# Strassen pairs of an FFN: weight loads ahead of state loads, states finished one pair later with four row buffers, and one two-bank PSUM tile for the first two products

## The chip, the cores and the metric

One core of one Trainium2 chip. The kernel is one decoder layer for a prompt of 512 tokens and 8 sample tokens (520 in all), in fp32. The metric is device time in microseconds of one execution; the time before is the median of three runs.

## The reference

```python
D_MODEL = 1024
...
    h2 = rmsnorm(x, norm2_w) * (1 + sc2) + sh2
    gt, up = jnp.split(h2 @ w_ffn_in, 2, axis=-1)
    x = x + g2 * ((jax.nn.silu(gt) * up) @ w_ffn_out)
```

The layer first has a pooling branch and a state-space branch; what matters here is its second half. `w_ffn_in` is 1024 x 5632: 22 columns of 128 for the gate and 22 for the up part. Beside the FFN the kernel finishes the recurrent states of the sample tokens, new state = old state x decay + outer product, which are an output (`ssm_sample`) and which nothing in the FFN reads:

```python
    def step(h, inp):
        st, dec = inp
        return h * dec[..., None, None] + st, h
```

## The kernel before

**fp32 from pieces.** A weight block of 128 x 1024 is loaded raw, cast on ScalarE to a high part (`hi`, or a name that ends in h) and subtracted from the raw one on VectorE for a low part (`lo`, or l). Every product takes three matmuls for each k of 128: hi·xh, hi·xl, lo·xh. Tokens stand in two halves of 260.

**Columns and pairs.** Column j of the FFN is its gate block g and its up block u. Columns 1 to 3, 8, 14, 20 and 21 are plain (`ffn`, L1446): 96 matmuls of 128x260. The 14 columns in `WINO` (4 to 19 without 8 and 14) are "Strassen pairs" (`wino`, L1554): g and u with the two token halves make a 2x2 block product, done with seven products of 12 matmuls, 84 in all. In PE's order they are g0, g1 (weights wg, made of g itself), x0 (wx), z0 (wz), y1 (wy), z1 (wz), y0 (wy). wx and wz come from sums and differences of quarters of g and u, which GpSimd makes in place in the raw buffers (L1530, L1531, L1536, L1537); wy is u as these steps have left it. The results are combined by adds on VectorE (L1573) into `f1` (u2), `f2` (u4) and the column's result tile `as`; the sum for y0, called the f2 add here, is the last. The copy of g0 to u2 is ScalarE's (L1577).

**What runs when.** In this stage every engine keeps the order in which the program is written (`manual_schedule`, L1314). During pair j the next pair's weights are made: `wino_third(j)` (wyuh, wyul for this pair's y1 and y0; one buffer each, so wyuh(j) waits for y0 of pair j-1), `wino_first(j+1)` (wxeh, wxel, two GpSimd steps, wghi, wglo, two GpSimd steps, then silu and multiply of column j-1, which were left over), `wino_second(j+1)` (wzhi, wzlo), and `pair_load(j+2)` issues the raw loads of g and u of 512 KB each on SP's queue. Raw buffers: three ("raw"), and one of their own for u of odd columns ("ur"). In the runs 9 to 13 and 15 to 19 one of the three holds the gate block of the plain column that follows (loaded by `ahead`, L1547), so two turn round.

**States.** A generator (`sample_states`) treats 32 blocks of state. A step A loads the block after next (L1343, L1344, on SP), multiplies on GpSimd (L1359) and makes the outer product on ScalarE (four instructions `ht`, L1365); a step B adds on VectorE (L1367) and stores by a GpSimd DMA (L1368). Each pair does an A behind the add of g1 and a B at its end; 13 blocks are treated in the pairs, the others after them. The blocks lie in unused result tiles as[19] to as[21], their vectors `bb` in as[17] and as[18].

**PSUM.** `main()` gives tiles of two banks (tag m, two buffers), `bank()` single banks (tag b, four buffers). In a pair x0 and y1 are the two halves of one main tile `m`; g0, g1, z0, z1 and y0 each take a bank.

Of the kernel before, what the change touches and what calls it, by code (L numbers as in the profile page):

```python
# [9 lines left out]
F32 = mybir.dt.float32  # L10
# [6 lines left out]
P = 128  # L17
T = 520
TP = 512
NS = 8  # L20
H2 = 260
# [23 lines left out]
NFS = 3  # L45
NU = 40
WINO = [j for j in range(4, 20) if j not in (8, 14)]
STATES = 17

SLICES = ((0, 1), (1, 3), (3, 5), (5, 7), (7, 8))  # L50
U_SH1, U_SC1, U_G1, U_SH2, U_SC2, U_G2 = (8 * i for i in range(6))
# [3 lines left out]
def tile_decoder(ctx: ExitStack, tc: tile.TileContext, I: dict, O: dict):  # L55
    nc = tc.nc
# [12 lines left out]
    def uid():  # L69
        count[0] += 1  # L70
        return count[0]
# [4 lines left out]
    def main():  # L76
        return pm.tile([P, 2, 512], F32, tag="m", name=f"m{uid()}")
# [8 lines left out]
    def halves(ap):  # L86
        return ap.rearrange("p (a b) -> p a b", a=2)
# [38 lines left out]
    def product(outs, w, k, xh, xl, first, last, c0=0):  # L126

        hi, lo = w
        for a, b, f, e in ((hi, xh, first, False), (hi, xl, False, False), (lo, xh, False, last)):
            for o, t0, t1 in outs:  # L130
                nc.tensor.matmul(o, a[:, k, c0 : c0 + P], b[:, t0:t1], start=f, stop=e)  # L131

    def both(ps):
        return [(ps[:, s, :H2], s * H2, (s + 1) * H2) for s in range(2)]
# [9 lines left out]
    def column(ws, xh, xl, between=None, outs=None):  # L144

        ps = outs or main()
        n = sum(w[0].shape[1] for w in ws)
        kk = 0
        for w in ws:
            for k in range(w[0].shape[1]):  # L150
                product(outs or both(ps), w, k, xh(kk), xl(kk), kk == 0, kk == n - 1)
                kk += 1
                if between:
                    between(kk)
        return ps
# [5 lines left out]
    G = {}  # L161
# [1163 lines left out]
    states = {}  # L1325
    NEARLY = STATES - WINO[0]

    def state_unit(n):

        return n // 4, 2 * (n % 4)  # L1330

    def state_load(n):
        if n >= 32:
            return
        g, b = state_unit(n)
        if n < NEARLY:
            h = G["as"][19 + n % 3][:, 0:TP].rearrange("p (b j n) -> p b j n", b=2, j=2)
            bb = G["as"][17 + n % 3 // 2][:, n % 3 % 2 * 256 :][:, 0:256].rearrange("p (b n) -> p b n", b=2)
        else:
            sp = G["hs"]  # L1340
            h = sp.tile([P, 2, 2, P], F32, tag="hs", name=f"hs{n}", bufs=4)
            bb = sp.tile([P, 2, P], F32, tag="bb", name=f"bb{n}", bufs=3)
        nc.sync.dma_start(out=h, in_=I["sssm"][g, :, b : b + 2])  # L1343
        nc.sync.dma_start(out=bb, in_=dbc[g, 0, b : b + 2].unsqueeze(0).broadcast_to([P, 2, P]))  # L1344
        states[n] = h, bb

    def sample_states():


        for n in range(2):  # L1350
            state_load(n)
        yield True
        for n in range(32):
            g, b = state_unit(n)
            if n >= NEARLY or n + 2 < NEARLY:
                state_load(n + 2)
            h, bb = states.pop(n)
            at = dtx[:, 1, 2 * g : 2 * g + 2, b : b + 2].rearrange("p j b -> p b j")
            nc.gpsimd.tensor_tensor(h, h, at.unsqueeze(3).broadcast_to([P, 2, 2, P]), ALU.mult)  # L1359
            t = G["ff"].tile([P, T], F32, tag="fs", name=f"ht{n}", bufs=NFS)[:, 0:TP]  # L1360
            t = t.rearrange("p (b j n) -> p b j n", b=2, j=2)
            for i in range(2):
                for j in range(2):
                    x = xds[:, 2 * g + j, b + i : b + i + 1]
                    nc.scalar.activation(t[:, i, j], bb[:, i], AF.Identity, bias=0.0, scale=x)  # L1365
            yield True
            nc.vector.tensor_tensor(h, h, t, ALU.add)  # L1367
            nc.gpsimd.dma_start(out=O["ssms"][g, :, b : b + 2], in_=h)  # L1368
            yield True

    def states_step():
        if "states" not in G:
            G["states"] = sample_states()
        return next(G["states"], False)

    class Scratch:

# [68 lines left out]
    def ffn(j):  # L1446
        def fn(wg, wu):
            xh, xl = (lambda k: G["hh"][:, k]), (lambda k: G["hl"][:, k])
            left()
            pg = column([wg], xh, xl)  # L1450
            if j + 1 in WINO:
                wino_first(j + 1)
                if WINO[0] < j < STATES:
                    states_step()
                pair_load(j + 2)
            pu = column([wu], xh, xl)
            if j + 1 in WINO:
                wino_second(j + 1)
                if WINO[0] < j < STATES:
                    states_step()  # L1460
            ffn_end(j, whole(pg), whole(pu))

        return fn
# [43 lines left out]
    def pair_load(n):  # L1507
        if n in WINO:
            u = I["wfi"][NF + n]
            if n % 2:  # L1510
                raw = G["we"].tile([P, KD, P], F32, tag="ur", name=f"ur{n}", bufs=1)
                nc.sync.dma_start(out=raw, in_=u)
            WW["raw", n] = load(I["wfi"][n]), raw if n % 2 else load(u)
        elif WINO[0] < n:
            ahead(len(W["made"]), 2)
# [5 lines left out]
    def wino_first(n, mult=None, silu=None):  # L1521


        if n in WINO:
            g, u = WW["raw", n]
            a11, a12, a21, a22 = g[:, 0:4], g[:, 4:8], u[:, 0:4], u[:, 4:8]
            WW["x", n] = [G["we"].tile([P, 4, P], F32R, tag=t, name=f"wx{t}{n}", bufs=2) for t in ("eh", "el")]
            split(*WW["x", n], a22)
            v = nc.gpsimd.tensor_tensor
            v(a22, a21, a22, ALU.add)  # L1530
            v(a21, a11, a21, ALU.subtract)  # L1531
        elif n <= WINO[-1]:
            ahead(len(W["made"]) + 1)
        if n in WINO:
            split(*wide(n, "g"), g)
            v(a11, a22, a11, ALU.subtract)  # L1536
            v(a12, a12, a11, ALU.subtract)  # L1537
        if silu:
            silu()
            mult()  # L1540

    def wino_second(n):

        if n in WINO:
            split(*wide(n, "z"), WW["raw", n][0])
        else:
            ahead(len(W["made"]) + 1, 1)  # L1547

    def wino_third(n):

        WW["y", n] = [G["we"].tile([P, KD, P], F32R, tag=t, name=f"wy{t}{n}", bufs=1) for t in ("uh", "ul")]
        split(*WW["y", n], WW.pop(("raw", n))[1])

    def wino(j):  # L1554
        def fn():
            f1, f2 = (G["ff"].tile([P, T], F32, tag="fs", name=f"fs{j}_{i}", bufs=NFS) for i in range(2))
            u2, u4 = f1[:, 0:H2], f2[:, H2:T]
            s = G["as"][j]
            sa, sb = s[:, 0:H2], s[:, H2:T]
            tt = G["tt"]  # L1560
            B = lambda r, c: (hblock("hh", r, c), hblock("hl", r, c))
            twice = lambda ap: ap.unsqueeze(1).broadcast_to([P, 2, H2])

            def mult(kind, half, x, o=None):
                hi, lo = WW[kind, j]
                o = bank()[:, 0:H2] if o is None else o
                for k in range(4):
                    q = 4 * half + k
                    for a, b, f, e in ((hi, x[0], k == 0, False), (hi, x[1], False, False), (lo, x[0], False, k == 3)):
                        nc.tensor.matmul(o, a[:, q], b[:, k], start=f, stop=e)  # L1570
                return o

            add = lambda out, a, b: nc.vector.tensor_tensor(out, a, b, ALU.add)  # L1573
            m = main()
            wino_third(j)
            wino_first(j + 1, *G.pop("left", ()))
            nc.scalar.copy(u2, mult("g", 0, B(0, 0)))  # L1577
            add(sa, mult("g", 1, B(1, 0)), u2)
            if j < STATES:
                states_step()  # L1580
            pair_load(j + 2)
            mult("x", 0, tt[3], m[:, 0, 0:H2])
            add(u2, mult("z", 0, tt[1]), u2)
            mult("y", 1, tt[0], m[:, 1, 0:H2])
            add(halves(f2), m[:, :, 0:H2], twice(u2))
            add(sb, mult("z", 1, B(1, 1)), u4)
            wino_second(j + 1)
            add(halves(f2), twice(mult("y", 0, tt[2])), halves(f2))
            if j < STATES:
                states_step()  # L1590
            G["left"] = (
                lambda: nc.vector.tensor_tensor(s, f2, s, ALU.mult),
                lambda: nc.scalar.activation(s, s, AF.Silu, bias=0.0, scale=1.0),
            )
            for kind in "gxyz":
                WW.pop((kind, j))

        return fn
# [238 lines left out]
```

## Time and profile before

| | us |
|---|---|
| median of three runs | 1111.27 (1110.36 to 1113.66) |
| the profiled execution | 1116.53 |
| its span in the trace | 1114.7 |
| pairs 4 to 7 (758.88 to 804.31) | 45.43 |
| pairs 9 to 13 (815.85 to 877.74) | 61.89 |
| pairs 15 to 19 (889.28 to 951.12) | 61.84 |

Times in rows are microseconds from the start of the span. PE is TensorE's matmuls, PEld its weight loads, DVE VectorE, ACT ScalarE, POOL GpSimd, SPq the queue of SyncE that issues the DMAs. A row of the timeline has start, duration, engine, line, operation, output<-input (buffer numbers left out), partitions x elements, and in brackets how long the engine had been idle and what ended it. PEclk is the granted clock of TensorE as a share of full speed. Two following starts on one engine can be closer than a duration, since an instruction's end overlaps the next one's start; where a chain on one engine is summed, the distance of starts is used.

### The profile page before, as it was taken

To read this page: it belongs to the slowest core of one execution; us is meant where nothing else is said; L and a number is where in the kernel's file an instruction comes from. 1 tells how busy PE (TensorE), PEld (TensorE's weight loads), DVE (VectorE), ACT (ScalarE), POOL (GpSimd) and SP (SyncE) were. 2 spreads that over 40 slices of the span, in tenths; PEclk is the share of its full clock that TensorE was granted. 3 is DMA by queue.
4 is the path that set the end of the run, shared out by engine and by line. 5 is a ranking of instruction groups with operands and counts; after the bars stand their busy time and mean duration, and the time that the engine had idled before them with its cause. 6 is when DMAs were issued, how large, how long until landed. Compare 5 with 4: busy or idle time off the path is not lost.

```text
span 1114.7 us, 22415 instructions
## 1 busy us (share of the span) xinstructions
PE 1068.8 (96%) x9163; PEld 1034.6 (93%) x9163; DVE 767.9 (69%) x1111; ACT 528.1 (47%) x952; POOL 319.8 (29%) x436
## 2 busy tenths in 40 slices
PE   7988999999999999999999999999998988999996
PEld 6987999999999999999998999899888988999996
DVE  5686787877877798788577645586756667845442
ACT  4358464664664534845333333633434444655430
POOL 1133344243243441000000000366555554032211
PEclk7998999999999999999999999999999999999998
DMA  9435454534634523454444354223443423386632
GB/s 355 187 91 173 132 161 123 190 106 132 190 106 133 164 92 124 151 171 144 152 142 156 128 187 175 79 102 130 152 160 126 157 95 99 106 269 212 210 95 77
DMA packets 63590, 165.36 MB, mean 148 GB/s; under 512 B 10880, under 2 KB 20608, under 8 KB 62720
## 3 DMA queue, kind: packets, MB, share of 16 engines
q1 hardware_dynamic: 60928, 155.54, 42.7%
q0 software_dynamic: 2560, 8.39, 1.9%
q8 instruction: 72, 1.18, 0.4%
q14 instruction: 30, 0.25, 0.1%
HBM read 151.05 MB, written 12.86 MB: 147 GB/s over the span
## 4 chain that ended last, share of the span: by engine, by line
PE 67%; DMA 8%; POOL 8%; DVE 6%; ACT 5%; issue 4%; SPq 1%; POOLq 0%; ACTq 0%; DVEq 0%
PE m L131 54%; PE b L131 4%; DMA raw<-in_wfi 2%; DMA raw<-in_win 2%; POOL raw L1536 2%; PE b L1570 1%; PE b L797 1%; POOL raw L1537 1%; DMA araw<-in_wada 1%; DMA ur<-in_wfi 1%; DMA araw<-in_wad 1%; PE b L772 1%; PE b L799 1%; ACT wzhi L158 1%; PE b L209 1%
## 5 line engine op out<-in xcount | busy, mean ns | idle before, releaser
L131 PE MATMUL m<-hh,whi 128*128 128x260 f32 (+2 forms) x1392 | 292.0, 289 | 3.6 <-ACT v L646 3.5
L131 PE MATMUL m<-hh,wlo 128*128 128x260 f32 (+2 forms) x1392 | 285.2, 285 | 0.4 <-DVE wlo L119 0.3
L131 PE MATMUL m<-hl,whi 128*128 128x260 f32 (+2 forms) x1392 | 285.0, 284 | 0.3 <-DVE hl L483 0.2
L119 DVE TENSOR_TENSOR wlo<-raw,whi 128x1024 fp32r<-128x1024 f32 (+1 forms) x138 | 175.5, 1276 | 79.9 <-ACT whi L118 77.1
L131 PEld LDWEIGHTS m<-hh,whi 128*128 128x128 f32 x1392 | 218.1, 190 | 9.6 <-ACT v L646 3.7
L131 PEld LDWEIGHTS m<-hh,wlo 128*128 128x128 f32 x1392 | 217.9, 190 | 0.8 <-DVE wlo L119 0.8
L131 PEld LDWEIGHTS m<-hl,whi 128*128 128x128 f32 x1392 | 217.8, 190 | 0.7 <-DVE hl L483 0.4
L118 ACT CAST whi<-raw 128x1024 fp32r<-128x1024 f32 (+1 forms) x138 | 140.4, 1022 | 155.8 <-PE m L131 125.5
L654 DVE SCALAR_TENSOR_TENSOR v<-xb,cwh,v 128x512 f32<-128x512 f32 x96 | 72.5, 756 | 39.9 <-POOL xb L641 19.6
L343 POOL TENSOR_TENSOR r<-me,mhalf 128x5 f32<-128x5 f32 (+2 forms) x6 | 6.4, 1065 | 279.4 <-DVE me L342 279.4
L645 ACT COPY xb<-m 128x520 f32<-128x520 f32 (+1 forms) x31 | 17.9, 577 | 81.7 <-PE m L131 81.7
L131 PE MATMUL m<-ah,whi 128*128 128x260 f32 x264 | 53.2, 283 | 0.0
L131 PE MATMUL m<-al,whi 128*128 128x260 f32 x264 | 53.2, 283 | 0.0
L131 PE MATMUL m<-ah,wlo 128*128 128x260 f32 x264 | 53.1, 282 | 0.0
L131 PE MATMUL m<-gh,whi 128*128 128x260 f32 x256 | 52.8, 288 | 0.0
L131 PE MATMUL m<-gl,whi 128*128 128x260 f32 x256 | 51.3, 282 | 0.0
L131 PE MATMUL m<-gh,wlo 128*128 128x260 f32 x256 | 51.3, 282 | 0.0
L818 POOL TENSOR_TENSOR h<-h,cc 128x1024 f32<-128x1024 f32 x16 | 39.0, 2437 | 27.9 <-DMA cc<-dbc 27.0
L158 ACT CAST wzhi<-raw 128x1024 fp32r<-128x1024 f32 x14 | 14.7, 1049 | 67.9 <-POOL raw L1537 67.9
L159 DVE TENSOR_TENSOR wzlo<-raw,wzhi 128x1024 fp32r<-128x1024 f32 x14 | 17.2, 1226 | 39.8 <-ACT wzhi L158 39.8
L288 DVE TENSOR_TENSOR ar<-araw,aw 128x1024 f32<-128x1024 f32 x24 | 29.4, 1224 | 18.6 <-ACT aw L287 18.4
L131 PEld LDWEIGHTS m<-gh,whi 128*128 128x128 f32 x256 | 39.2, 188 | 2.4 <-PE b L303 1.1
(389 smaller groups left out, 2562.0 us busy)
## 6 DMA issues: line engine op xcount, KB each, us to landing
raw<-in_win SPq DMA_DIRECT2D x73, 512.0 KB, 4.8
raw<-in_wfi SPq DMA_DIRECT2D x36, 512.0 KB, 4.3
araw<-in_wada SPq DMA_DIRECT2D x24, 512.0 KB, 4.1
h<-in_sssm SPq DMA_DIRECT2D x16, 512.0 KB, 4.0
raw<-in_wssd SPq DMA_DIRECT2D x16, 512.0 KB, 3.4
raw<-in_wfo SPq DMA_DIRECT2D x16, 512.0 KB, 3.9
araw<-in_wad SPq DMA_DIRECT2D x6, 1024.0 KB, 14.6
hs<-in_sssm SPq DMA_DIRECT2D x19, 256.0 KB, 4.3
```

The lines of the kernel that those rows point to most:

```text
L118: nc.scalar.copy(hi, raw)
L119: nc.vector.tensor_tensor(lo, raw, hi.bitcast(F32), ALU.subtract)
L131: nc.tensor.matmul(o, a[:, k, c0 : c0 + P], b[:, t0:t1], start=f, stop=e)
L158: nc.scalar.copy(hi, src)
L159: nc.vector.tensor_tensor(lo, src, hi.bitcast(F32), ALU.subtract)
L209: nc.tensor.matmul(ps[32 * i : 32 * i + 32, 0:n], sc[:, k], raw[:, n * i : n * i + n], start=first, stop=last)
L288: nc.vector.tensor_tensor(r, raws[n], w1, ALU.subtract)
L645: nc.scalar.copy(shape(xb[:, 3 + t0 : 3 + t1]), o)
L654: nc.vector.scalar_tensor_tensor(v[:, 0:TP], xb[:, k : k + TP], w(k), v[:, 0:TP], ALU.mult, ALU.add)
L772: nc.tensor.matmul(o, bm[:, cc], xde[:, cc].rearrange("p h d -> p (h d)"), start=True, stop=True)
L818: nc.gpsimd.tensor_tensor(h0, h0, cc.unsqueeze(2).broadcast_to([P, 4, 2, P]), ALU.mult)
L1536: v(a11, a22, a11, ALU.subtract)
```

## The change

1. `pair_load(j + 2)` moves to the front of a pair's work, ahead of `wino_first(j + 1)` and the state's step A, so on SP the weight loads stand ahead of the state loads.
2. The states take `states_unit(j)`: behind the add of g1, step B of the last pair's block and then step A of the next. Row buffers are as[18] to as[21] by turns, `bb` has a pool of its own with three buffers, and `STATES` is 18: 14 blocks in the pairs.
3. g0 and g1 go to the two halves of a main tile `mg`; the banks are left to z0, z1 and y0.
4. `wino_second(j + 1)` comes behind the f2 add of y0.

```diff
-STATES = 17
+STATES = 18
...
-            h = G["as"][19 + n % 3][:, 0:TP].rearrange("p (b j n) -> p b j n", b=2, j=2)
-            bb = G["as"][17 + n % 3 // 2][:, n % 3 % 2 * 256 :][:, 0:256].rearrange("p (b n) -> p b n", b=2)
+            h = G["as"][18 + n % 4][:, 0:TP].rearrange("p (b j n) -> p b j n", b=2, j=2)
+            bb = G["we"].tile([P, 2, P], F32, tag="bb", name=f"bb{n}", bufs=3)
...
+    def states_unit(j):
+
+        if WINO[0] < j <= STATES:
+            states_step()
+        if WINO[0] <= j < STATES:
+            states_step()
...
             if j + 1 in WINO:
                 wino_first(j + 1)
-                if WINO[0] < j < STATES:
-                    states_step()
                 pair_load(j + 2)
+                states_unit(j)
             pu = column([wu], xh, xl)
             if j + 1 in WINO:
                 wino_second(j + 1)
-                if WINO[0] < j < STATES:
-                    states_step()
...
-            m = main()
+            m, mg = main(), main()
             wino_third(j)
+            pair_load(j + 2)
             wino_first(j + 1, *G.pop("left", ()))
-            nc.scalar.copy(u2, mult("g", 0, B(0, 0)))
-            add(sa, mult("g", 1, B(1, 0)), u2)
-            if j < STATES:
-                states_step()
-            pair_load(j + 2)
+            nc.scalar.copy(u2, mult("g", 0, B(0, 0), mg[:, 0, 0:H2]))
+            add(sa, mult("g", 1, B(1, 0), mg[:, 1, 0:H2]), u2)
+            states_unit(j)
             mult("x", 0, tt[3], m[:, 0, 0:H2])
             add(u2, mult("z", 0, tt[1]), u2)
             mult("y", 1, tt[0], m[:, 1, 0:H2])
             add(halves(f2), m[:, :, 0:H2], twice(u2))
             add(sb, mult("z", 1, B(1, 1)), u4)
+            add(halves(f2), twice(mult("y", 0, tt[2])), halves(f2))
             wino_second(j + 1)
-            add(halves(f2), twice(mult("y", 0, tt[2])), halves(f2))
-            if j < STATES:
-                states_step()
```

Lines behind L1372 stand a few lines further down in the changed kernel (L1570 is L1574, L1573 and L1577 are L1577 and L1582).

**PE, from g0 to g1 of pair 10.** Names end in a number; b580 and b581 are banks, m575 is the two-bank tile `mg`, hh2 and hl2 are the tokens' high and low parts. A bracket lists the semaphores that an instruction waits for, by the engine that raises them. Before:

```order
L1570 MATMUL b580_10257<-hl2_8188,wghi10_10117 128x260
L1570 MATMUL b580_10257<-hh2_8187,wglo10_10118 128x260
L1570 MATMUL b581_10271<-hh2_8187,wghi10_10117 128x260 [waits DVE_49]
L1570 MATMUL b581_10271<-hl2_8188,wghi10_10117 128x260
L1570 MATMUL b581_10271<-hh2_8187,wglo10_10118 128x260
```

After:

```order
L1574 MATMUL m575_10240<-hl2_8188,wghi10_10123 128x260
L1574 MATMUL m575_10240<-hh2_8187,wglo10_10124 128x260
L1574 MATMUL m575_10240<-hh2_8187,wghi10_10123 128x260 [waits Activation_49]
L1574 MATMUL m575_10240<-hl2_8188,wghi10_10123 128x260
L1574 MATMUL m575_10240<-hh2_8187,wglo10_10124 128x260
```

The products stand in the same order; the first matmul of g1 waited for VectorE (a bank to be emptied) and now waits for ScalarE. The count that it waits for is that of the copy of g0 to u2, the same for which VectorE's add of g1 waits.

**ScalarE, pair 12 in the changed kernel.** The copy is fs12_0<-m588; in front of it are this pair's wyuh, the next pair's casts and the left-over silu of column 11, behind it the state's four instructions and wzhi.

```order
L158 CAST wyuh12_10509<-raw577_10247 128x1024
L158 CAST wxeh13_10515<-ur13_10379 128x512
L158 CAST wghi13_10521<-raw583_10381 128x1024
L1594 ACTIVATE as11_8986<-as11_8986 128x520
L1582 COPY fs12_0_10505<-m588_10508 128x260
L1365 ACTIVATE ht8_10561<-bb8_10291,xds_94 128x128 x4
L158 CAST wzhi13_10633<-raw583_10381 128x1024
```

Before, these seven stand in the same order; the copy read a bank, and ht read bb from as[18].

**VectorE, from the end of pair 9 into pair 10.** fs9_1 is f2 of pair 9, as9 its result, as21 and as18 hold states. Before:

```order
L1573 TENSOR_TENSOR as9_8984<-b577_10202,fs9_1_10105 128x260
L159 TENSOR_TENSOR wzlo10_10217<-raw569_10043,wzhi10_10216 128x1024
L1573 TENSOR_TENSOR fs9_1_10105<-b578_10220,fs9_1_10105 128x520
L1367 TENSOR_TENSOR as21_8996<-as21_8996,ht5_10154 128x512
L159 TENSOR_TENSOR wyul10_10240<-raw570_10045,wyuh10_10239 128x1024
L159 TENSOR_TENSOR wxel11_10244<-ur11_10159,wxeh11_10243 128x512
L159 TENSOR_TENSOR wglo11_10250<-raw575_10161,wghi11_10249 128x1024
```

After:

```order
L1577 TENSOR_TENSOR as9_8984<-b572_10205,fs9_1_10106 128x260
L1577 TENSOR_TENSOR fs9_1_10106<-b573_10219,fs9_1_10106 128x520
L159 TENSOR_TENSOR wzlo10_10234<-raw565_10035,wzhi10_10233 128x1024
L159 TENSOR_TENSOR wyul10_10242<-raw566_10037,wyuh10_10241 128x1024
L159 TENSOR_TENSOR wxel11_10250<-ur11_10113,wxeh11_10249 128x512
L159 TENSOR_TENSOR wglo11_10256<-raw570_10115,wghi11_10255 128x1024
```

The f2 add, which waits for y0, stands ahead of wzlo(10), and the state's add has gone to the next pair, behind the add of g1.

## The prediction

> **What bounds the kernel now.** First the page: where busy time goes, and whether one engine has all of it.
>
> ```profile
> PE 1068.8 (96%) x9163; PEld 1034.6 (93%) x9163; DVE 767.9 (69%) x1111; ACT 528.1 (47%) x952; POOL 319.8 (29%) x436
> ```
>
> TensorE (PE) is busy for 96% of the 1114.7 us span, so an edit that neither adds nor removes matmuls can only win or lose PE's idle time. The change touches columns 4 to 19 of the FFN, so I ask next for busy time by stretch: pairs 4 to 7, plain column 8, pairs 9 to 13, pairs 15 to 19, and last a short piece of pair 18.
>
> ```profile
> core 0: us, PE busy (x) PEld busy (x) DVE busy (x) ACT busy (x) POOL busy (x), PEclk, DMA share, GB/s
> 758.88:804.31 45.43, 41.99 (x339) 40.77 (x337) 32.04 (x40) 22.26 (x40) 26.35 (x20) 1.00 0.40 131
> 804.31:815.85 11.54, 11.54 (x98) 11.54 (x97) 5.47 (x8) 3.49 (x7) 5.79 (x5) 1.00 0.65 214
> 815.85:877.74 61.89, 55.11 (x423) 52.65 (x422) 43.84 (x52) 28.00 (x50) 33.18 (x28) 0.97 0.37 127
> 889.28:951.12 61.84, 54.95 (x422) 52.67 (x421) 40.51 (x51) 25.11 (x39) 29.36 (x23) 0.97 0.30 99
> 930.40:933.81 3.41, 3.41 (x18) 3.41 (x17) 2.00 (x3) 2.51 (x3) 0.73 (x1) 0.50 0.00 0
> ```
>
> The plain column keeps PE full: eight products of 12 matmuls in 11.54 us, so one product takes 1.44 us and a pair's seven 10.1 us. The 14 pairs take 45.43 + 61.89 + 61.84 = 169.2 us, where 14 x 10.1 = 141: PE waits for some 28 us. For what, the groups of weight loads say (the last column is PE's idle time before the group and what ended it).
>
> ```profile
> L1570 PEld LDWEIGHTS b<-hh,wghi 128*128 128x128 f32 x112 | 22.3, 200 | 7.2 <-DVE as L1573 7.1
> L1570 PEld LDWEIGHTS b<-t1h,wzlo 128*128 128x128 f32 x56 | 10.5, 188 | 3.9 <-DVE wzlo L159 3.9
> L1570 PEld LDWEIGHTS m<-t0h,wyul 128*128 128x128 f32 x56 | 10.5, 188 | 6.9 <-DVE wyul L159 6.9
> L1570 PEld LDWEIGHTS b<-t2h,wyuh 128*128 128x128 f32 x56 | 10.5, 188 | 4.4 <-ACT fs L1577 4.4
> ```
>
> There are two kinds of wait. The products g0 and y0 wait for a PSUM bank (until the add of g1, or the copy at L1577, has emptied one); z0 and y1 wait for weights. One turn of the weights, pair 4 into pair 5, on VectorE:
>
> ```profile
> 764.20 0.68 DVE L159 TENSOR_TENSOR wxel<-ur,wxeh 128x512 fp32r<-128x512 f32 x1
> ...
> 772.41 1.23 DVE L159 TENSOR_TENSOR wzlo<-raw,wzhi 128x1024 fp32r<-128x1024 f32 x1 [4.03 <-ACT wzhi L158]
> 773.56 0.69 DVE L1573 TENSOR_TENSOR fs<-b,fs 128x520 f32<-128x520 f32 x1
> 774.17 0.68 DVE L1367 TENSOR_TENSOR as<-as,ht 128x512 f32<-128x512 f32 x1
> 774.77 1.22 DVE L159 TENSOR_TENSOR wyul<-ur,wyuh 128x1024 fp32r<-128x1024 f32 x1
> 775.90 0.68 DVE L159 TENSOR_TENSOR wxel<-raw,wxeh 128x512 fp32r<-128x512 f32 x1
> ```
>
> From wxel to wxel is 11.70 us. GpSimd's four subtractions, wzhi, wzlo, the f2 add of y0, the state's add, wyul and wxel follow one another, and the change takes the f2 add (0.61) and the state's add (0.60) out from between. That is what it can win. Now what it adds.
>
> **The new wait.** In the built program the first matmul of g1 waits for ScalarE, for the very count that the add of g1 waits for: the copy of g0 to u2. g0 and g1 are now halves of one tile, and a write to the tile waits for a read of it. Before, g1 had a bank of its own, and of the pair's products only y0 came after that copy. So the question is how late the copy is. It stands on ScalarE behind wyuh(j), wxeh(j+1), wghi(j+1) and silu(j-1). Pairs 11 and 12, with PE's starts of each:
>
> ```profile
> 840.54 0.39 PE L1570 MATMUL b<-hh,wghi 128*128 128x260 f32 x1 [0.64 <-DVE as L1573]
> 854.45 0.39 PE L1570 MATMUL b<-hh,wghi 128*128 128x260 f32 x1 [1.79 <-DVE as L1573]
> ```
>
> ```profile
> 848.53 0.62 ACT L158 CAST wxeh<-raw 128x512 fp32r<-128x512 f32 x1 [3.83 <-DMA raw<-in_wfi]
> 849.06 1.05 ACT L158 CAST wghi<-raw 128x1024 fp32r<-128x1024 f32 x1
> 850.01 0.63 ACT L1593 ACTIVATE as<-as 128x520 f32<-128x520 f32 x1
> 850.54 0.35 ACT L1577 COPY fs<-b 128x260 f32<-128x260 f32 x1
> ...
> 862.35 1.05 ACT L158 CAST wghi<-raw 128x1024 fp32r<-128x1024 f32 x1 [3.26 <-DMA raw<-in_wfi]
> 863.31 0.64 ACT L1593 ACTIVATE as<-as 128x520 f32<-128x520 f32 x1
> 863.85 0.36 ACT L1577 COPY fs<-b 128x260 f32<-128x260 f32 x1
> ```
>
> The copy ends 10.35 and 9.76 us after g0's first matmul, and g0 takes 1.44. Before, PE used that time for five products; now everything behind g0 waits. And the load that holds the copy up isn't late for SP's order, which the change does improve: it waits for a buffer.
>
> ```profile
> 843.78 1.23 DVE L159 TENSOR_TENSOR wzlo<-raw,wzhi 128x1024 fp32r<-128x1024 f32 x1 [1.43 <-ACT wzhi L158]
> 844.92 0.69 DVE L1573 TENSOR_TENSOR fs<-b,fs 128x520 f32<-128x520 f32 x1
> ...
> 857.65 1.22 DVE L159 TENSOR_TENSOR wzlo<-raw,wzhi 128x1024 fp32r<-128x1024 f32 x1 [1.39 <-ACT wzhi L158]
> 858.80 0.69 DVE L1573 TENSOR_TENSOR fs<-b,fs 128x520 f32<-128x520 f32 x1
> ```
>
> ```profile
> 858.91 0.33 SPq L109 DMA_DIRECT2D raw<-in_wfi  x1
> ```
>
> SP issues the load 0.04 us after wzlo(12) ends at 858.87. Of three raw buffers one holds the preloaded weight of the next plain column in each run of five pairs, so two turn round, and the load for pair 13 goes where g(12) was until wzlo(12) had read it. The change then moves wzlo(j) on VectorE behind the f2 add, which waits for the last matmul of pair j-1. That closes a ring that PE itself stands in.
>
> **The sum, runs of five pairs.** Even pair j, from the end of y0(j-1): semaphores to VectorE and back to PE 0.3 (my estimate: two or three steps of the size of 858.87 to 858.91, rounded up), f2 add 0.61 (773.56 to 774.17), then from wzlo's start to the copy's end 864.21 - 857.65 = 6.56, then six products 6 x 1.44 = 8.64: 16.1 us. Odd pair: the load that waits is u's, and wxeh, which reads u, stands ahead of wghi: 850.89 - 843.78 = 7.11 in place of 6.56: 16.65. Last pair (13, 19): nothing to load, ScalarE has one wyuh (0.95), a cast of the plain column (0.95), silu (0.53) and the copy (0.36) from the end of y0 on: 2.8 + 0.3 + 8.64 = 11.7. First pair (9, 15): its turn begins in the plain column, as before:
>
> ```profile
> 824.19 0.36 ACT L1577 COPY fs<-b 128x260 f32<-128x260 f32 x1
> 898.29 0.36 ACT L1577 COPY fs<-b 128x260 f32<-128x260 f32 x1
> ```
>
> 824.55 - 815.85 = 8.70, + 8.64 = 17.3; and 898.65 - 889.28 = 9.37, + 8.64 = 18.0. The runs come to 17.3 + 16.1 + 16.65 + 16.1 + 11.7 = 77.9 (before 61.9: +16.0) and 18.0 + 16.1 + 16.65 + 16.1 + 11.7 = 78.6 (before 61.8: +16.7).
>
> **Pairs 4 to 7.** Here no raw buffer is held, and loads land in time. Pair 4:
>
> ```profile
> 758.88 0.28 PE L1570 MATMUL b<-hh,wghi 128*128 128x260 f32 x1
> ```
>
> ```profile
> 761.19 0.60 ACT L1397 ACTIVATE as<-m 128x520 f32<-128x520 f32 x1
> 764.09 0.38 ACT L1577 COPY fs<-b 128x260 f32<-128x260 f32 x1
> ```
>
> g0 now takes the PSUM tile that silu of plain column 3 reads until 761.79 (2.9 us of wait), and g1 the copy's end at 764.47: 5.6 + 8.64 = 14.2. Pairs 5 and 6: wyuh waits for the end of y0 (its tile has one buffer), then 0.95 + 0.53 + 0.95 + 0.53 + 0.36 = 3.3 to the copy's end, + 0.3 + 8.64 = 12.3 each; pair 7 as 13, 11.7. Sum 50.5, before 45.4: +5.1.
>
> **What lies beside.** The four row buffers, bb in a pool of its own and the state's add one pair later move work of 1 to 1.3 us an instruction off VectorE's urgent stretch; with PE waiting 2 to 6 us a pair for the copy, VectorE and GpSimd have that slack anyway, so I count 0. GpSimd's multiply still stands behind its subtractions. State loads behind weight loads on SP: 0 for the same reason, since the state is needed a pair later. One state more lies in the pairs and one fewer behind them, where the page shows PE at nine tenths or more: 0, at most its add, multiply and scaling, some 3 us, either way. Own banks for z0, z1, y0: y0 no longer waits for a bank, which the sums above hold already.
>
> **The clock.** The stretch 930.40 to 933.81 follows a stall of PE and shows PEclk 0.50, with 18 matmuls recorded in 3.41 us; at the plain column's pace 28 fit, so a hit costs up to 10 x 0.12 = 1.2 us.
>
> ```profile
> 913.39 0.39 PE L1570 MATMUL b<-t2h,wyuh 128*128 128x260 f32 x1 [1.19 <-ACT fs L1577]
> 929.02 0.39 PE L1570 MATMUL b<-hh,wghi 128*128 128x260 f32 x1 [1.78 <-DVE as L1573]
> ```
>
> The stall that it follows lasted 1.78 us; one of 1.19 wasn't followed by a slow stretch. The sums make eleven stalls of 2 to 7 us (four in each run of five, three in the first run): 0 to 13 us, and part of a slow stretch may fall into the stall itself, so I take half, 6 us. [...]
>
> **Total.** 16.0 + 16.7 + 5.1 + 6 = +43.8. The profiled execution took 1116.5 us (span 1114.7), 5.3 over the median of the runs shown, 1111.27, and within its own few tenths of a per cent of them; 1116.5 + 43.8 - 5.3 = 1155 us.
>
> **Rivals.** *The wait is there but the loads come in time* (SP's new order gets a free buffer sooner): every pair but the first of a run is then 12.3, the last 11.7: 50.5 + 66.0 + 66.7 = 183.2, +14, so 1125. For it: weight loads now go ahead of state loads. Against: 858.91, issued 0.04 us after wzlo. *The wait doesn't bite* (the chip or the build lets g1 go on before the copy): then the chain of weights bounds the pairs as before, and with wzlo behind the f2 add little is won: -2 to +2, 1111. Against: the wait is in the built program. [...] *Faster*: the copy is ready when g0 ends. It has to end within 1.44 us of g0's start, so wghi(j+1) must be cast before pair j begins and wyuh must not stand ahead. Then the ring of 11.70, less the two adds, decides: 14 x 10.5 = 147 against 169, -22, 1089. Against: all of the copies quoted end 5.6 us or more after g0's start. *Slower still*: clock hits at every stall (+7), and the loads that PE waits for share the queues with the state loads issued behind them; the lone load took 862.35 - 858.91 = 3.44, and the page's median for such loads is 4.3 us, so six of them cost +5: 1167.
>
> ```profile
> raw<-in_wfi SPq DMA_DIRECT2D x36, 512.0 KB, 4.3
> ```
>
> **How the numbers follow.** The forecast has 0.80, loads in time 0.09, no bite 0.05, faster 0.03, above 1172 0.03. The range is the forecast's own: down to 1137 without the clock (-6) and with three of the six middle pairs' loads in time (-3 x 4, from 16 to 12), up to 1167 of the last rival, + 3 for the state and 2 for scatter: 1172. The cases outside it hold 0.20. About 0.3% is what a measurement of this kernel can tell from no change; faster by more than that 0.03, within 0.05, slower 0.92.
>
> **What would show it.** Right: in the groups, PE's idle time before b<-hh,wghi goes, and a group of matmuls of wghi into m waits some 40 us or more, ended by ScalarE's fs copy; runs of five take 73 to 82 us; slow clock stretches in most pairs; PE idle before wyul and y0's wyuh near nothing. Wrong: g1 follows g0 without a gap, or wghi's cast is not preceded by a wait for raw<-in_wfi.

## The result and the profile after

| | before | after |
|---|---|---|
| median | 1110.98 us (four runs, 1110.36 to 1113.66) | 1166.97 us (four runs, 1165.45 to 1167.33) |
| the profiled execution | 1116.53 us | 1166.78 us |
| its span | 1114.7 us | 1164.9 us |

The change makes the kernel 4.96% slower: the ratio is 1.0496, 95% interval 1.0477 to 1.0516. The time lies in the range that was given (1137 to 1172), 12 us above the forecast.

The page of the changed kernel, first its busy times:

```profile
PE 1077.9 (93%) x9163; PEld 1046.4 (90%) x9163; DVE 773.6 (66%) x1111; ACT 530.2 (46%) x952; POOL 323.1 (28%) x436
```

The instruction counts are those of before, and VectorE, ScalarE and GpSimd are busy as long as they were, to 6 us. Of the 50 us of span, PE stands idle for 41 more than before (87.0 against 45.9) and is busy for 9 more, at a lower clock (granted on average over the span: 0.960 against 0.980). The three stretches of pairs, with the same columns as before (the first starts at the end of plain column 3, since g0 of pair 4 now waits):

```profile
757.35:808.57 51.22, 42.90 (x338) 41.80 (x337) 33.05 (x41) 23.64 (x42) 26.87 (x20) 0.97 0.40 133
820.19:905.19 85.00, 59.80 (x421) 58.75 (x421) 43.80 (x53) 27.97 (x50) 31.93 (x26) 0.82 0.33 109
916.80:999.68 82.88, 59.66 (x421) 58.60 (x421) 42.19 (x51) 25.49 (x41) 29.24 (x23) 0.84 0.24 80
```

45.43, 61.89 and 61.84 us have become 51.22, 85.00 and 82.88: +49.9 us, the whole difference of the spans. The mean clock falls from 0.97 and 0.97 to 0.82 and 0.84 in the runs of five. The groups of weight loads say what PE waits for; this is the only group of a pair in the changed kernel with a wait of note:

```profile
L1574 PEld LDWEIGHTS m<-hh,wghi 128*128 128x128 f32 x112 | 25.8, 230 | 60.2 <-ACT fs L1582 57.1 <-ACT as L1404 2.9
```

The four waits of before (7.2 for a bank, 3.9 for wzlo, 6.9 for wyul, 4.4 for the copy ahead of y0) are gone. In their place stand 57.1 us for the copy at L1582, and 2.9 us for silu of column 3. One turn, the end of pair 10 and pair 11, followed through VectorE, SP, ScalarE and PE:

```profile
856.16 0.70 DVE L1577 TENSOR_TENSOR fs<-b,fs 128x520 f32<-128x520 f32 x1 [1.01 <-PE b L1574]
856.78 1.22 DVE L159 TENSOR_TENSOR wzlo<-raw,wzhi 128x1024 fp32r<-128x1024 f32 x1
```

```profile
858.02 0.33 SPq L109 DMA_DIRECT2D raw<-in_wfi  x1
858.46 0.36 SPq L1343 DMA_DIRECT2D as<-in_sssm  x1
858.87 0.43 SPq L1344 DMA_DIRECT2D bb<-dbc  x1
```

```profile
862.14 0.62 ACT L158 CAST wxeh<-raw 128x512 fp32r<-128x512 f32 x1 [4.99 <-DMA raw<-in_wfi]
862.66 1.04 ACT L158 CAST wghi<-raw 128x1024 fp32r<-128x1024 f32 x1
863.61 0.63 ACT L1594 ACTIVATE as<-as 128x520 f32<-128x520 f32 x1
864.15 0.36 ACT L1582 COPY fs<-m 128x260 f32<-128x260 f32 x1
```

```profile
864.56 0.58 PE L1574 MATMUL m<-hh,wghi 128*128 128x260 f32 x1 [7.00 <-ACT fs L1582]
```

The f2 add starts when PE has finished y0 of pair 10; wzlo follows it; the load starts 0.02 us after wzlo has ended (858.00) and frees the buffer; ScalarE casts what has landed 4.12 us later; the copy ends at 864.51, and 0.05 us later g1 starts, after PE has stood for 7.00 us. Every step of the ring is in the rows, in the order that was forecast.

### The profile page after: what moved, and what is told of

It reads as the page before. It is cut to its first block, busy times and chain, and to the rows that moved or that the text cites. A ratio compares the mean times of both kernels' runs of the same rounds, so it can differ in the third digit from the quotient of the medians.

```text
span 1164.9 us, 22402 instructions
## 1 busy us (share of the span) xinstructions
PE 1077.9 (93%) x9163; PEld 1046.4 (90%) x9163; DVE 773.6 (66%) x1111; ACT 530.2 (46%) x952; POOL 323.1 (28%) x436
## 4 chain that ended last, share of the span: by engine, by line
PE 71%; DMA 9%; ACT 7%; DVE 6%; issue 4%; POOL 3%; SPq 0%; POOLq 0%; ACTq 0%; DVEq 0%
PE m L131 50%; PE m L1574 6%; PE b L1574 4%; DMA araw<-in_wada 4%; PE b L131 3%; DMA raw<-in_wfi 2%; PE b L797 2%; DVE ar L288 1%; PE b L772 1%; DMA araw<-in_wad 1%; PE b L799 1%; DMA raw<-in_win 1%; DVE wzlo L159 1%; ACT aw L287 1%; PE b L209 1%
## 5 line engine op out<-in xcount | busy, mean ns | idle before, releaser
L1574 PE MATMUL m<-hh,wghi 128*128 128x260 f32 x112 | 38.8, 346 | 56.7 <-ACT fs L1582 54.0
L1574 PEld LDWEIGHTS m<-hh,wghi 128*128 128x128 f32 x112 | 25.8, 230 | 60.2 <-ACT fs L1582 57.1
L1365 ACT ACTIVATE ht<-bb,xds 128x128 f32<-128x128 f32 x128 | 40.9, 391 | 20.8 <-DVE as L1593 20.6
L1577 DVE TENSOR_TENSOR fs<-b,fs 128x260 f32<-128x260 f32 (+1 forms) x28 | 15.8, 564 | 38.8 <-PE b L1574 38.8
```

## The experiments

Two theories stood against each other. A: the loss is the wait of g1 for the copy of g0, through the tile that both now share, and the copy is late because it stands on ScalarE behind casts of a load that waits for a raw buffer. B: the loss comes from the new order on the queues (wzlo behind the f2 add, the loads, the states). Every run is timed against the kernel before on the same chip; the ratios are to that.

### Parting the tile from the order

**e1_g1_bank**: g1 gets a bank of its own, the rest of the change stays.

```diff
-            add(sa, mult("g", 1, B(1, 0), mg[:, 1, 0:H2]), u2)
+            add(sa, mult("g", 1, B(1, 0)), u2)
```

> The change, but g1 writes a bank of its own; g0 keeps its tile. Theory A (the loss is g1's wait for a late copy, through the shared tile): the wait of some 58 us before wghi goes, the clock stays up, time within 1095 to 1118 us. Theory B (the loss is the new order: wzlo behind the f2 add, loads, states): still above 1140 us.

Measured: 1113.45 us, ratio 1.0006 (0.9995 to 1.0016). One line takes the loss away. In the groups of weight loads g0 (into its tile m) keeps its wait for silu, and g1 (into a bank b) waits for nothing but its bank:

```profile
L1574 PEld LDWEIGHTS b<-hh,wghi 128*128 128x128 f32 x56 | 11.1, 198 | 1.6 <-DVE as L1577 1.6
L1574 PEld LDWEIGHTS m<-hh,wghi 128*128 128x128 f32 x56 | 11.1, 197 | 4.1 <-ACT as L1404 3.0 <-ACT fs L1582 0.9
```

**e2_only_tile**: the kernel before with the shared tile and nothing else.

```diff
-            m = main()
+            m, mg = main(), main()
...
-            nc.scalar.copy(u2, mult("g", 0, B(0, 0)))
-            add(sa, mult("g", 1, B(1, 0)), u2)
+            nc.scalar.copy(u2, mult("g", 0, B(0, 0), mg[:, 0, 0:H2]))
+            add(sa, mult("g", 1, B(1, 0), mg[:, 1, 0:H2]), u2)
```

> The kernel before, with nothing but g0 and g1 in one two-bank tile. A: PE waits for ScalarE's copy in every pair; since wzlo still stands ahead of the f2 add the load comes sooner than in the change, so a pair takes between 12.3 us (load in time) and 16 (load late): 1125 to 1155 us. B: within 5 us of 1111.

Measured: 1155.97 us, ratio 1.0384 (1.0369 to 1.0400), 1 us above A's range. The wait ahead of wghi is there too:

```profile
L1570 PEld LDWEIGHTS m<-hh,wghi 128*128 128x128 f32 x112 | 25.7, 229 | 47.6 <-ACT fs L1577 44.6 <-ACT as L1397 3.0
```

The tile alone brings +43 us. The other 11 us, from here to the change, come with the new order on top of the tile. They lie where the load is late: ahead of g1 in the first four pairs of each run of five, PE stands for 34.0 us in all in e2 and for 46.6 us in the change. That this is the ring through the f2 add (in e2 wzlo doesn't wait for it) is argued, not shown by a run of its own.

**e3_no_tile**: the change without the tile.

```diff
-            m, mg = main(), main()
+            m = main()
...
-            nc.scalar.copy(u2, mult("g", 0, B(0, 0), mg[:, 0, 0:H2]))
-            add(sa, mult("g", 1, B(1, 0), mg[:, 1, 0:H2]), u2)
+            nc.scalar.copy(u2, mult("g", 0, B(0, 0)))
+            add(sa, mult("g", 1, B(1, 0)), u2)
```

> The change without the two-bank tile: all five products that had a bank before have one again, in the new order. A: 1095 to 1120 us; beside e1 it tells what the own banks are worth once the shared tile is gone (0 to 5 us). B: above 1140 us.

Measured: 1111.56 us, ratio 0.9989 (0.9978 to 1.0000). A new order alone that wins next to nothing is a question of its own; its stretches and its waits answer it:

```profile
755.60:799.27 43.67, 41.24 (x338) 40.63 (x338) 34.09 (x41) 22.66 (x41) 26.86 (x20) 1.00 0.41 139
810.81:871.91 61.10, 54.84 (x422) 53.16 (x422) 45.51 (x53) 27.03 (x49) 32.65 (x26) 0.94 0.42 140
883.45:945.01 61.56, 53.43 (x422) 51.10 (x422) 43.59 (x51) 24.91 (x41) 29.92 (x23) 1.00 0.33 108
```

```profile
L1574 PEld LDWEIGHTS b<-t1h,wzlo 128*128 128x128 f32 x56 | 10.5, 188 | 6.7 <-DVE wzlo L159 6.5
L1574 PEld LDWEIGHTS b<-t2h,wyuh 128*128 128x128 f32 x56 | 10.5, 188 | 9.4 <-ACT fs L1582 9.4
```

Pairs 4 to 7 go from 45.43 to 43.67 us, the runs of five stay at 61. The wait for wyul (6.9 us before) is gone, and that for the bank of y0, which the late copy frees, has grown from 4.4 to 9.4, that for wzlo from 3.9 to 6.7. If A is right, the runs of five are held by the load that waits for a raw buffer, with the tile or without it; e5 below tries that. Beside e3, e1 with own banks for z0, z1 and y0 is 2 us slower, not faster: it pays the 3.0 us for silu in pair 4.

**e4_copy_first**: the tile stays, and the copy goes to the head of ScalarE's work in a pair.

```diff
+            nc.scalar.copy(u2, mult("g", 0, B(0, 0), mg[:, 0, 0:H2]))
             wino_third(j)
             pair_load(j + 2)
             wino_first(j + 1, *G.pop("left", ()))
-            nc.scalar.copy(u2, mult("g", 0, B(0, 0), mg[:, 0, 0:H2]))
```

> The change with its shared tile, but ScalarE's copy of g0 is written ahead of wyuh, wxeh, wghi and silu. A: g1 still waits for the copy, but only for its own 0.36 us and the semaphores, some 0.7 us a pair; no stall long enough for the clock; 1100 to 1122 us. If it were the tile as such, and not the copy's place behind the load: above 1140 us. B: above 1140 us.

Measured: 1122.46 us, ratio 1.0086 (1.0070 to 1.0101): 44 of the 56 us are gone with the tile in place, so it is the copy's place in the queue that made the wait long. The tile still costs 11 us beside e3. The end of the expected range was just missed, and the working behind it by more: PE waits 19.3 us for the copy, where 14 times 0.7 is some 10, and in four pairs of the runs of five 10 to 17 matmuls go at half pace, where no stall was to be long enough for that.

```profile
L1574 PEld LDWEIGHTS m<-hh,wghi 128*128 128x128 f32 x112 | 23.0, 206 | 27.7 <-ACT fs L1579 19.3 <-issue 5.1 <-ACT as L1404 3.0
```

The copy still stands behind wzhi(j), which is written in pair j-1. In pair 5 that costs nothing, in pair 10 wzhi waits for GpSimd, and g1 with it:

```profile
773.67 0.38 ACT L1579 COPY fs<-m 128x260 f32<-128x260 f32 x1 [0.34 <-PE m L1574]
...
830.91 1.05 ACT L158 CAST wzhi<-raw 128x1024 fp32r<-128x1024 f32 x1 [5.33 <-POOL raw L1541]
831.86 0.37 ACT L1579 COPY fs<-m 128x260 f32<-128x260 f32 x1
```

```profile
774.10 0.39 PE L1574 MATMUL m<-hh,wghi 128*128 128x260 f32 x1 [0.47 <-ACT fs L1579]
...
832.28 0.58 PE L1574 MATMUL m<-hh,wghi 128*128 128x260 f32 x1 [2.38 <-ACT fs L1579]
```

### The raw buffer

The other half of A is that the copy was late because of a buffer. It is set free by loading the gate block of the next plain column only when pair 12 or 18 asks for it (`pair_load` does so anyway), so that three raw buffers turn round in the runs of five:

```diff
     def wino_second(n):
...
         else:
-            ahead(len(W["made"]) + 1, 1)
+            ahead(len(W["made"]) + 1, int(n > WINO[-1]))
```

This edit goes onto e3 (**e5_buffer_free**), onto the kernel before (**e6_before_free**), onto the change (**e7_after_free**) and onto e1 (**e8_g1_bank_free**).

> The order of the change without the shared tile (as in e3_no_tile), and the gate block of the next plain column is loaded only when pair 12 or 18 asks for it, so three raw buffers turn round in the runs of five. Theory A now says that in e3_no_tile these runs are bound by the raw buffer (load behind wzlo): each middle pair falls from 12 to 15 us to some 11, runs of five from 61 to 54 or 56, time 1097 to 1103 us. Theory C (they are bound by GpSimd and VectorE anyway): 1109 to 1113.

> The kernel before with nothing but that later load of the plain column's gate block. A: its pairs then go at the 11.0 to 12.0 us of pairs 5 to 7, 5 x 11.8 = 59 in place of 61.9: 1103 to 1109 us; what e5 wins beyond it is the new order's. C: no change, 1109 to 1114.

> The change as it is, shared tile included, with that later load. A: the copy comes at wyuh, two casts and silu behind y0, a pair takes 12.3 us as pairs 5 and 6 do, the stalls fall to 2 us and most slow clock stretches go: 1124 to 1138 us, which parts the loss of the change into copy order (some 20) and buffer with clock (some 35). B or a load that isn't behind the buffer: 1155 to 1170.

> As e5_buffer_free, but g0 keeps a two-bank tile of its own and g1, z0, z1, y0 take the four banks (as in e1_g1_bank). A: y0 waits for no bank; pair 4 pays 2.9 us for silu of column 3 ahead of g0: 1096 to 1104, within 3 us of e5.

| | us | ratio to before (95%) |
|---|---|---|
| e5_buffer_free | 1096.31 | 0.9858 (0.9841 to 0.9876) |
| e6_before_free | 1103.29 | 0.9918 (0.9898 to 0.9937) |
| e7_after_free | 1126.43 | 1.0128 (1.0100 to 1.0155) |
| e8_g1_bank_free | 1097.04 | 0.9870 (0.9845 to 0.9895) |

e6, e7 and e8 lie where A put them; e5 is 0.7 us faster than A's range, and no run is where B or C put it. e7 is the change with nothing but that later load, and takes 40 us less. Its stretches come to 53.6, 62.9 and 63.5 us, PE's wait for the copy falls from 57.1 to 24.2 us, and ScalarE's casts no longer wait for a load (pair 11):

```profile
L1574 PEld LDWEIGHTS m<-hh,wghi 128*128 128x128 f32 x112 | 23.2, 207 | 27.4 <-ACT fs L1582 24.2 <-ACT as L1404 3.0
```

```profile
848.81 0.61 ACT L158 CAST wxeh<-raw 128x512 fp32r<-128x512 f32 x1
849.33 1.04 ACT L158 CAST wghi<-raw 128x1024 fp32r<-128x1024 f32 x1
```

```profile
757.38:810.97 53.59, 44.67 (x339) 43.68 (x338) 33.20 (x41) 23.53 (x42) 26.83 (x20) 0.94 0.40 131
822.58:885.45 62.87, 54.84 (x422) 53.79 (x422) 43.89 (x53) 27.57 (x50) 34.66 (x26) 0.95 0.42 145
897.06:960.54 63.48, 56.39 (x422) 55.34 (x421) 42.29 (x51) 25.07 (x41) 31.93 (x23) 0.92 0.28 99
```

The clock's part came otherwise than A had it. The granted clock in the runs of five is 0.95 and 0.92 (0.82 and 0.84 in the change), but the slow stretches did not mostly go: seven are left, of 3.0 to 3.4 us each, and they cost some 1.5 us apiece.

e5 is faster than both kernels. Its runs of five fall from 61 to 53 us, against a floor of 50.5 (five pairs of 10.1), and one wait is left in the pairs:

```profile
811.62:864.74 53.12, 50.97 (x422) 50.55 (x421) 45.50 (x53) 26.62 (x50) 34.62 (x27) 1.00 0.45 152
876.28:929.05 52.77, 50.97 (x422) 50.56 (x421) 43.50 (x51) 24.59 (x42) 32.07 (x24) 1.00 0.33 120
```

```profile
L1574 PEld LDWEIGHTS b<-t1h,wzlo 128*128 128x128 f32 x56 | 10.5, 188 | 7.6 <-DVE wzlo L159 7.6
```

e8 against e5 says what banks of their own for z0, z1 and y0 are worth once the copy is in time: nothing on balance (1097.04 against 1096.31). e8 pays 3.0 us for silu in pair 4, and its wait for wzlo is 2.5 us shorter; no run parts the two.

### What in the new order wins

e6 and e5 differ by 7 us: by the loads' place, the states and wzlo's place. Two runs take one of these back out of e5, and e5 runs again beside them.

**e9_wzlo_first**:

```diff
+            wino_second(j + 1)
             add(halves(f2), twice(mult("y", 0, tt[2])), halves(f2))
-            wino_second(j + 1)
```

> As e5_buffer_free, but wzlo(j+1) stands ahead of the f2 add of y0 again, as before. The ring of the weights (wxel, GpSimd's four, wzhi, wzlo, wyul, wxel) takes the f2 add's 0.61 us back in. A: if that ring is what still differs between e6_before_free (1103) and e5_buffer_free (1096), 1098 to 1101 us. Rival: the place of wzlo is worth nothing by itself: 1095 to 1097.5.

**e10_states_old**: the old row buffers and `bb`, `STATES` 17, step A behind the add of g1 and step B at the pair's end:

```diff
-            states_unit(j)
+            if j < STATES:
+                states_step()
...
             wino_second(j + 1)
+            if j < STATES:
+                states_step()
```

> As e5_buffer_free, but the states as before: three row buffers, a state's add at the end of its own pair (behind wzlo, ahead of wyul). A: the state's add (0.60 us) and its wait for GpSimd and ScalarE are back in the ring: 1098 to 1102 us. Rival: states moved for nothing: 1095 to 1097.5.

> e5_buffer_free once more, on the chip of e9 and e10: 1095 to 1098 us.

Measured: e11 1094.21 us, ratio 0.9829 (0.9804 to 0.9855); e10 1095.17, 0.9834 (0.9816 to 0.9853); e9 1102.50, 0.9902 (0.9883 to 0.9921). e11 lies 0.8 us below what was expected. Moving the states is worth nothing that can be measured: e10 came out at its rival's time, not at A's 1098 to 1102. Putting wzlo behind the f2 add is worth 8 us, and e9 is 1.5 us slower than A's range. It is not one f2 add of 0.61 us in each of the 14 pairs: in the traces eight pairs take 0.6 to 1.2 us longer in e9 than in e11 and the others 0.3 at most, 6.3 us in all (the spans are 1099.8 and 1092.9). In e9 waits for wzhi and wyul come back beside that for wzlo:

```profile
L1574 PEld LDWEIGHTS b<-t1h,wzhi 128*128 128x128 f32 x56 | 10.5, 188 | 1.7 <-ACT wzhi L158 1.7
L1574 PEld LDWEIGHTS b<-t1h,wzlo 128*128 128x128 f32 x56 | 10.5, 188 | 9.3 <-DVE wzlo L159 9.3
L1574 PEld LDWEIGHTS m<-t0h,wyul 128*128 128x128 f32 x56 | 10.5, 188 | 2.2 <-DVE wyul L159 2.2
```

e9 is also the kernel e6 with the loads ahead and the states moved, and stands to the kernel before as e6 does (0.9902 and 0.9918, the intervals overlap): these two together, from which the change has its name, are worth nothing that can be measured.

## Why the prediction held, and where its sizes were off

**The wait.** Forecast: g1 waits for the copy of g0 through the shared tile. Shown by e1 (the wait goes with the tile), e2 (it comes with the tile alone) and e4 (it shrinks when the copy is early). The rival in which the wait doesn't bite is out. The two halves lie in two banks, and the trace of the change shows the wait all the same: g1 starts 0.05 us behind the copy (864.56 and 864.51). What was built guards the tile, not the bank: in e1, where g1 has a bank that is not of this tile, it waits 1.6 us in all, for VectorE to empty that bank, and not for the copy.

**The load behind wzlo.** Forecast: the load is late for a buffer, and wzlo behind the f2 add closes the ring. That the buffer makes it late is shown by e7 and by the rows of pair 11; what the f2 add costs in this ring no run shows by itself. Pair by pair the working fits: from g0 to the next pair's g0, pairs 5 and 6 of the changed kernel take 12.20 and 12.25 us (12.3 forecast), and pairs 10 and 12 take 17.86 and 17.85, of which some 1.8 go with the lower clock: 16.1, as forecast.

The rival "the loads come in time" had 183.2 us for the 14 pairs and 1125 us; e7, which makes them come in time, has 53.59 + 62.87 + 63.48 = 179.9 us and 1126.43. The mechanism of the rival is right, but that its time is so near is partly luck. It left the first pairs of the runs of five at 17.3 and 18.0 us, and they take 11.4 each in e7, since their load comes in time too; it counted nothing for the clock, and seven pairs of e7 take 13.7 us in place of 12.3, at half pace for a while. The two errors, 12 and 10 us, cancel. The one such pair whose clock stayed up takes 12.25.

**The sum.** The 14 pairs were to take 50.5 + 77.9 + 78.6 = 207.0 us at full clock, and 6 for the clock. They took 219.1. Matmuls at about half pace (starts 0.19 to 0.24 us apart in place of 0.12) number some 170 in these stretches of the trace and lose some 17 us in all, so the rest is about 202: the waits were put 5 us too high. The first pairs of the runs of five account for it. In the changed kernel the copy of pair 9 is this row:

```profile
826.61 0.37 ACT L1582 COPY fs<-m 128x260 f32<-128x260 f32 x1
```

It ends 6.8 us after g0's start at 820.19, where 8.70 was taken from before, and that of pair 15 is sooner by 2.8 us in the same way: wzlo(9) ends 1.1 us behind g0's start in place of 3.2, because the turn of the plain column ahead shifted against PE, which the working had left where it was. The load of pair 11, 4.12 us with state loads beside it and not 3.44, goes the other way by 0.7.

The clock term is the one that was most mis-sized: 6 us as the prediction put it, some 17 measured. It counted part of a stretch of 3.41 us for each stall; each of the eight stalls of 4.87 to 7.00 us was followed by 3.4 to 5.8 us at half pace, as in pair 11:

```profile
864.20:867.60 3.40, 3.04 (x14) 3.04 (x15) 3.40 (x2) 0.30 (x2) 3.24 (x3) 0.50 0.00 0
867.60:871.00 3.40, 3.40 (x22) 3.40 (x22) 1.74 (x3) 1.76 (x5) 3.32 (x3) 0.68 0.00 0
```

14 and 22 matmuls where 28 fit: eight such stalls cost some 2 us each. Waits 5 us too high and a clock term 11 too low leave 6: these two errors hid each other in part. The runs of five, 85.0 and 82.9 us, lie above the 73 to 82 that the prediction named as a sign of being right; without the clock's some 8 us in each they would lie within.

**From the span to the median.** I took 5.3 us off, because the profiled execution of before was that much above its median. The changed kernel's profiled execution lies on its median (1166.78 and 1166.97). The offset belonged to one execution of before, not to the profile; this step is nearly half of the 12 us by which the forecast was low.

**What lies beside.** Counted at 0: the states are so (e10 against e11: 1 us, inside the intervals). Own banks come to 1 us on balance (e8 against e5). Wzlo behind the f2 add was taken as part of the ring, and for the case without the wait as "little is won". With the buffer as it was, that is so (e3: -0.1%); with the buffer free it wins the 8 us of e9 against e11.

## What to carry to other kernels

In this program two products in one PSUM tile shared its waits, though they lay in two banks: the write to one half waited for the reader of the other, 57.1 us in the 14 pairs of the change and 44.6 in e2. So ask how late that reader stands in its engine's order before putting them together. When an order is improved and nothing moves, look for the resource under it: here an early load held one of three buffers, and one changed argument with the better order brought what neither brought alone (-1.4 to -1.7%, against -0.1% and -0.8%). A term for the lower clock is worked out from all stalls that the new wait makes, and at the length that such stalls have (here eight of 4.87 to 7.00 us, at some 2 us each).

## What was not expected of the hardware

Two like stalls did not always have like consequences for the clock. In the changed kernel g1 waits 1.85 us in pair 5 and 1.90 in pair 6, and the clock stays up behind both (1.00 from 776.40 to 779.80 and from 787.90 to 791.30); in the kernel before 1.78 us were followed by 3.41 us at 0.50. In e7, PE stood still for 1.85 to 1.91 us eight times, ahead of g1; seven of these waits were followed by matmuls at half pace for some 3.0 to 3.4 us, and one, which ended at 864.97, by none. The first row here is the stretch behind the wait of pair 5 in the changed kernel, the two others are stretches behind such waits in e7:

```profile
776.40:779.80 3.40, 3.40 (x30) 3.40 (x29) 3.40 (x4) 0.75 (x3) 3.32 (x2) 1.00 0.91 314
```

```profile
776.41:779.82 3.41, 3.41 (x19) 3.41 (x18) 3.41 (x4) 1.28 (x4) 3.25 (x3) 0.54 0.98 367
865.13:868.54 3.41, 3.41 (x29) 3.41 (x30) 3.41 (x5) 0.42 (x2) 3.14 (x2) 1.00 0.93 306
```

So waits of 1.8 to 1.9 us were enough for the lower clock in some places and not in others. What decides it is not shown: no run was made for it.
